# Weight low halves wholly on VectorE for every batch of a decoder layer, with the emission order that follows

## The chip, the cores and the metric

The kernel runs on one NeuronCore of a Trainium2 chip. The metric is the device time of one execution in microseconds; the kernel before has 2865.8 us as the median of three runs (2864.34 to 2872.69). The engines are named as the profile names them: PE is TensorE (its weight loads stand apart as PEld), DVE is VectorE, ACT is ScalarE, POOL is GpSimd, and SP issues all the DMAs.

## The reference, cut to what matters

One decoder layer on 2048 prompt tokens and 8 x 4 sample tokens, in float32. A modulated RMSNorm feeds one input projection; its columns go to three token mixers (SSD, RWKV-7, S5); their outputs are joined and projected, added to the residual, and a second modulated norm feeds a squared-ReLU MLP of width 4096.

```
h    = rmsnorm(x) * (1 + sc1) + sh1
proj = h @ w_in
y    = concat(ssd(proj), rwkv(proj), s5(proj))
x    = x + g1 * (y @ w_out)
h2   = rmsnorm(x) * (1 + sc2) + sh2
x    = x + g2 * (relu(h2 @ w1)**2 @ w2)
```

## The kernel before

Tokens go in four batches b = 0..3 of 512; batch 2 carries the 32 sample tokens too, so its matrix products go in two pieces of 272 columns where the others go in one of 512. Features lie on the partitions. Each large product is made in float32 precision from rounded operands: a weight `w` and an activation `x` are each split into a rounded high half and a low half (`lo = w - hi`), and three matmuls are summed, hi by hi, hi by lo and lo by hi. These are the "GEMM" matmuls of this text; in the rows they read `bk<-arena_r` (`arena_r` is the rounded part of SBUF, `arena` the rest, `bk` a PSUM bank). There are 11,344 such matmuls in the program (64 of them belong to S5) and 2,812 others, mostly float32 and small, which belong to the mixers, the norms and the modulation; "small matmuls" here.

A weight tile of 128 x 1024 comes by one DMA and is used as two halves of 128 x 512. `wprep` has ACT write the high half, `wlow` (line 716) makes the low half. `WS.POOL` says how many of its 512 columns POOL subtracts; the rest is DVE's. It is 288 during all four input projections and for batches 0 and 1 of the second part, and 0 for batches 2 and 3 (line 2538). So 462 halves are split between the two engines: 176 of the input projections and 286 of batches 0 and 1 after them.

The program first does the input projections of the four batches (`in_proj`), and then for each batch the output projection and the MLP (`out_proj0` or `out_proj`, `mlp`). The mixers run as generators beside all of this. The output projection of a batch needs the mixers' output of that batch: it is stored to DRAM tiles named `sph` and read back by `y_gen`, which splits it in two halves for the GEMM.

Nothing reorders the instructions on the chip: each engine runs its list as written. The order is set while the program is written, by `Plan`, which keeps a rough clock for each engine and books a cost for each instruction (in `Eng`). For DVE and POOL it books, for n columns:

```
cost = 72 + 1.04 * n + (30 if ps else 0)                       # DVE
cost = 60 + (2.4 if op == "tensor_tensor" else 0.9) * n        # POOL
```

`pump` (line 314) lets the generators write their next instructions, and passes one over while a booked clock is too far ahead:

```
if max(clk["DVE"], clk["ACT"]) > clk["PE"] + lag or clk["POOL"] > clk["PE"] + 2 * lag:
    continue
```

`gemm` (line 779) calls `wprep` and `wlow` one or two halves ahead of use and calls `pump` after every four matmuls; `wait_for` and `until` pump until a flag is there.

Of the kernel before, what the change touches and what calls it, by code (L numbers as in the profile page):

```python
# [110 lines left out]


class Plan:
    """Rough clocks of the engines while the program is written; they only decide the order in which it is written."""

    LAT = {"PE": 197.0, "DVE": 128.0, "ACT": 143.0, "POOL": 85.0, "SP": 0.0}
    U = 32
# [27 lines left out]

    IDS = {"PE": 1, "DVE": 2, "ACT": 3, "POOL": 4, "SP": 5}

# [41 lines left out]
class Eng:  # L189
# [3 lines left out]
    def __getattr__(self, op):  # L193
# [3 lines left out]
        def call(*a, **k):  # L197
# [34 lines left out]
            elif name == "ACT":  # L232
                cost = 95 + 0.833 * n
            elif name == "POOL":
                cost = 60 + (2.4 if op == "tensor_tensor" else 0.9) * n
# [12 lines left out]
def layer_kernel(ctx: ExitStack, tc: tile.TileContext, d, o, dbg=None):  # L248
    nc = tc.nc
    plan = Plan()  # L250
    V, S, P, T, Q = (Eng(plan, *x) for x in (("DVE", nc.vector), ("ACT", nc.scalar), ("POOL", nc.gpsimd), ("PE", nc.tensor), ("SP", nc.sync)))

# [30 lines left out]

    ctx.enter_context(tc.manual_schedule())

    # ------------------------------------------------------------ plumbing
    gens = []
    done = set()

# [5 lines left out]
    def spawn(g, rank=5, ready=0.0):  # L295
        x = Gen(g, rank)
        x.ready = ready
        gens.append(x)
        gens.sort(key=lambda q: q.rank)
        return x  # L300
# [13 lines left out]
    def pump(budget=1500, idle=False):  # L314
# [3 lines left out]
        while go and clk["PE"] < limit:  # L318
            go = False
            for x in list(gens):  # L320
                if x.ready > clk["PE"] + (60 if idle or x.rank < MRANK else -tune[0]):
                    continue
                lag = LAG1 if x.rank < 0.5 else LAG3 if crit[0] else tune[1]
                if max(clk["DVE"], clk["ACT"]) > clk["PE"] + lag or clk["POOL"] > clk["PE"] + 2 * lag:
                    continue
# [122 lines left out]
    def bc(ap, k, n):  # L448
        return ap.unsqueeze(k).to_broadcast([*ap.shape[:k], n, *ap.shape[k:]])

    # ------------------------------------------------------------ constants
    cst = M.get(C_N)
    vec = M.get(V_N)
    cin = M1.get(72)
# [52 lines left out]
    s5dec = M.get(512)  # L507
    V.memset(s5h.f, 0.0)

    # ------------------------------------------------------------ small helpers  # L510
    def rsqrt(v, n, p=128):
        t_, y_, h_ = (grab(n, AM) for _ in range(3))
        t, y, h = t_.f[0:p], y_.f[0:p], h_.f[0:p]
        ts(t.bitcast(I32), v.bitcast(I32), 1, None, ALU.logical_shift_right)
        ts(h, v, -27.0 / 1024, None, ALU.mult)
        ts(y.bitcast(I32), t.bitcast(I32), -1.0, float(0x5F3759DF), ALU.mult, ALU.add)
        tt(t, y, y, ALU.mult)
        tt(t, t, v, ALU.mult)
        stt(t, t, -10.0 / 3, t, ALU.add, ALU.mult)
        yield 0  # L520
        stt(y, t, 5.0, y, ALU.add, ALU.mult)
        tt(t, y, y, ALU.mult)
        tt(t, t, h, ALU.mult)
        stt(y, t, 0.5625, y, ALU.add, ALU.mult)
        yield 0
        free(t_, h_)
        return y_
# [77 lines left out]
        ts(dv(D_A, 8), dv(D_A, 8), -1.0, None, ALU.mult)  # L605
        done.add("A")

    # ------------------------------------------------------------ adaLN
    mod = M.get(48 * 9)
    modv = mod.v("p (m s) -> p m s", m=48)  # L610
    G1 = M.get(72)
# [68 lines left out]
            yield  # L680
            yield from finish()

    # ------------------------------------------------------------ weights
    NWH = 4
    wring = [(MR.get(512), MR.get(512)) for _ in range(NWH)]
    wbuf = M.get(1024 * NRB)
# [3 lines left out]
    class WS:  # L690
# [1 line left out]
        ready = 0  # L692
        low = 0
        pos = 0
        POOL = 288

    def wload(upto):
        while WS.loaded < min(upto, len(wseq)):
# [5 lines left out]
    def whalves(i):  # L704
        hi, lo = wring[i % NWH]
        return hi, lo, wraw[i // 2 % NRB][:, 512 * (i % 2):512 * (i % 2) + 512]
# [9 lines left out]
    def wlow(upto):  # L716
        while WS.low < min(upto, WS.ready):
            i = WS.low
            hi, lo, raw = whalves(i)
            c = 512 - WS.POOL  # L720
            tt(lo.r[:, 0:c], raw[:, 0:c], hi.f[:, 0:c], ALU.subtract)
# [137 lines left out]
                fn(bk, BT - c0, c1 - c0, BT, True)  # L859
            gput(bk)  # L860

    # ------------------------------------------------------------ token mixers, first stage
    def store(dst, src):
        Q.dma_start(dst, src)

# [307 lines left out]
        ub.free()  # L1173
        done.add(("u", b, i))

    # ------------------------------------------------------------ S5
    LWS = -0.30326532985631671

    def s5_setup():
# [369 lines left out]
        yf.free()  # L1549
        done.add(("s5", b))  # L1550

    # ------------------------------------------------------------ SSD
    def ssd_chunk(b, c):
        smp = c == 4
        n = 32 if smp else 128
# [159 lines left out]
        for c in cs:  # L1715
            yield from admit(ssd_chunk(b, c), C_SSD, R_SSD(b))

    # ------------------------------------------------------------ RWKV, second stage
    def rw_pre(b):
        hasS = b == SB  # L1720
        nch = 9 if hasS else 8
# [370 lines left out]
        if b == SB:  # L2092
            spawn(ssd_gen(b, [4]), R_SMP)

    # ------------------------------------------------------------ main line
    def mix_flags(b):
        fl = [("s5", b)]
        for c in range(5 if b == SB else 4):
            fl += [("ssd", b, c), ("rw", b, c)]
        return fl  # L2100
# [242 lines left out]
    def out_proj0(acts):  # L2343
        xs = []
        for k in range(2):
            load_x(0, k, xs)
        for c in range(4):
            until(("ssd", 0, c))
        wait_for(lambda: len(acts) >= 4, "acts")
        for m in range(8):  # L2350
            if m < 6:
                load_x(0, m + 2, xs)
            resid(xs[m], gemm([(h.r, l.r) for h, l in acts[0:4]], False, acts[0:4] if m == 7 else ()), modv[:, GA1 + m], False)
            pump()
        acc = [mal(W), 0]
        wait_for(lambda: len(acts) == 8, "acts")
        for m in range(8):
            resid(xs[m], gemm([(h.r, l.r) for h, l in acts[4:8]], False, acts[4:8] if m == 7 else ()), modv[:, GA1 + m], False)
            square(xs[m], acc, BT)
            pump()  # L2360
        new = []
        spawn(norm2_gen(xs, acc, False, new), 0)
        return xs, new

    def out_proj(b, acts):
        hasS = b == SB
        n = W if hasS else BT
        xs = []
        for k in range(2):
            load_x(b, k, xs)  # L2370
        for fl in mix_flags(b):
            until(fl)
        acc = [mal(W), 0]
        pair = gemm2(acts, hasS)
        for m in range(8):
            if m < 6:
                load_x(b, m + 2, xs)
            got = next(pair) if m < 2 else gemm([(h.r, l.r) for h, l in acts], hasS, acts if m == 7 else ())
            resid(xs[m], got, modv[:, GA1 + m], hasS)
            square(xs[m], acc, n)  # L2380
            crit[0] = m == 7
            pump()
        new = []
        spawn(norm2_gen(xs, acc, hasS, new), 0)
        return xs, new
# [44 lines left out]
    def w2_chunk(b, xs, hid, ms=range(8), acc=None):  # L2430
        hasS = b == SB
        n = W if hasS else BT
        while tails:
            x = tails.pop(0)
            if x in gens:
                for _ in x.g:
                    pass
                gens.remove(x)
        until(("ada", 23))
        hid = [hid[j] for j in range(4)]  # L2440
        hp = [(h.r, l.r) for h, l in hid]
        for m in ms:
            got = gemm(hp, hasS)
            resid(xs[m], got, modv[:, GA2 + m], hasS)
            if acc is not None:
                square(xs[m], acc, n)
            pump()
        if m == 7:
            for h, l in hid:
                free(h, l)  # L2450
# [31 lines left out]
    def final_gen(b, xs, acc):  # L2482
        hasS = b == SB
        out = []
        while acc[1] < 8:
            yield
        yield
        yield from stats_end(acc[0::2], 1.0 / 1024, 1e-6, hasS, out)
        yield
        yield from bcast_gen(out, hasS)  # L2490
        yield
        bk, b2 = out
        n = W if hasS else BT
        for k in range(8):
            stt(xs[k].f[:, 0:BT], xs[k].f[:, 0:BT], vv(V_GF + k), bk, ALU.mult, ALU.mult)
            if hasS:
                stt(xs[k].f[:, BT:W], xs[k].f[:, BT:W], vv(V_GF + k), b2[:, 0:32], ALU.mult, ALU.mult)
            Q.dma_start(o["y"][k, :, boff[b]:boff[b] + n], xs[k].f[:, 0:n])
            if k % 2:
                yield 0  # L2500
        MB.put(bk)
        if b2 is not None:
            MB.put(b2)
        free(*xs)
        done.add(("final", b))

    # ------------------------------------------------------------ run
    first4 = [4, 0, 5, 1, 6, 2, 7, 3]
    nxt = [[]]
    ys = []  # L2510
# [24 lines left out]
    until(("ada", 11))  # L2535
    last = None
    for b in range(NB):
        WS.POOL = 0 if b > 1 else 288
        tune[:] = MARGIN2, LAG4
        xs, acts = out_proj(b, ys) if b else out_proj0(ys)  # L2540
        for _ in rest:
            pass
        if last is not None:
            w2_chunk(*last[0:3], range(HOLD, 8), last[3])
            spawn(final_gen(last[0], last[1], last[3]), 0.4)
        ys = []
        hid, acc = mlp(b, xs, acts, ys)
        last = (b, xs, hid, acc)
# [11 lines left out]
        dbg(nc, locals())  # L2560


# [1 line left out]
def _consts():  # L2564
    c = np.zeros((128, C_N), np.float32)
    i = np.arange(128)
# [161 lines left out]
```

## Time and profile before

| | |
|---|---|
| median of three runs | 2865.8 us (2864.34 to 2872.69) |
| profiled execution, span from first to last instruction | 2863.7 us |
| PE busy | 2739.5 us, 96% |
| DVE busy | 1967.3 us, 69% |
| ACT busy | 1142.5 us, 40% |
| POOL busy | 653.5 us, 23% |

The profile gives no time beside the span; the median of the runs lies 2.1 us above it. By the time of the first load of `w_out` (`in_w_out`, 785.81 us on SP's queue) the output projection of batch 0 is about to start; POOL has nothing more to do after about 1,950 us. A row of the timeline has a start, a duration, an engine, an operation and its shapes; instructions of one kind that follow each other are merged (x2).

### The profile page before, as it was taken

The numbers are of one execution on the slowest core, as the hardware profiler recorded it, in microseconds if no ns is written. First come the engines' busy times: TensorE is split into PE (matmuls) and PEld (weight loads), VectorE is DVE, ScalarE is ACT, GpSimd is POOL, SyncE is SP. The second block draws the span as 40 slices with busy tenths as digits, with TensorE's granted clock in tenths as the row PEclk, the third lists the DMA queues.
The fourth block names the chain that finished last, engine by engine and source line by source line (L and its number), as shares of the span: only waits on it lengthen the run. The fifth ranks groups of instructions, "written<-read, shape, count | busy, mean of one in ns | idle before, by whom it ended". The sixth has DMA issues, their size and how long they took to land.

```text
span 2863.7 us, 45369 instructions
## 1 busy us (share of the span) xinstructions
PE 2739.5 (96%) x16651; PEld 2265.7 (79%) x16651; DVE 1967.3 (69%) x4567; ACT 1142.5 (40%) x2153; POOL 653.5 (23%) x829
## 2 busy tenths in 40 slices
PE   7999889999999999999999999999999999999997
PEld 4677778877777777777777777778899999888886
DVE  6988996887997877666676778676653535643434
ACT  4354443454335432233443432334534344433342
POOL 1234432233442233322323343321000000000000
PEclk9999999999999999999999999999999999999999
DMA  8467656446553444433434364334222223232222
GB/s 284 155 213 252 201 163 198 164 155 215 170 191 115 144 125 155 146 115 97 159 129 135 118 188 142 120 118 151 96 89 89 89 89 133 82 126 96 99 93 74
DMA packets 302667, 406.26 MB, mean 142 GB/s; under 512 B 85604, under 2 KB 197348, under 8 KB 302444
## 3 DMA queue, kind: packets, MB, share of 16 engines
q1 hardware_dynamic: 302444, 403.36, 42.8%
q8 instruction: 131, 2.15, 0.3%
q14 instruction: 92, 0.75, 0.1%
HBM read 329.67 MB, written 73.62 MB: 141 GB/s over the span
## 4 chain that ended last, share of the span: by engine, by line
PE 62%; DVE 9%; issue 2%; ACT 1%; DMA 1%; POOL 0%; SPq 0%; DVEq 0%; POOLq 0%; ACTq 0%
PE bk L198 62%; DVE arena L198 7%; DVE arena_r L198 2%; ACT arena L198 1%; ACT arena_r L198 1%; DMA arena<-sph 0%; DMA arena<-spk 0%; POOL arena L198 0%; DMA arena<-in_w_out 0%; POOL arena_r L198 0%; DMA arena<-spl 0%; SPq L198 0%; DVEq L198 0%; DVEq L2724 0%; POOLq L198 0%
## 5 line engine op out<-in xcount | busy, mean ns | idle before, releaser
L198 PE MATMUL bk<-arena_r 128*128 128x512 f32 (+1 forms) x11344 | 2284.7, 358 | 61.7 <-DVE arena_r L198 41.5
L198 PEld LDWEIGHTS bk<-arena_r 128*128 128x128 f32 x11344 | 1843.9, 190 | 397.9 <-DVE arena_r L198 65.4
L198 DVE TENSOR_TENSOR arena_r<-arena,arena_r 128x224 fp32r<-128x224 f32 (+2 forms) x981 | 577.7, 610 | 416.9 <-ACT arena_r L198 410.6
L198 ACT ACTIVATE arena_r<-arena 128x512 fp32r<-128x512 f32 (+1 forms) x976 | 581.5, 627 | 468.4 <-PE bk L198 394.3
L198 POOL TENSOR_TENSOR arena_r<-arena,arena_r 128x288 fp32r<-128x288 f32 (+1 forms) x530 | 510.7, 976 | 1055.2 <-ACT arena_r L198 933.2
L198 ACT ACTIVATE arena<-bk 128x512 f32<-128x512 f32 (+8 forms) x619 | 271.9, 459 | 1008.5 <-PE bk L198 798.3
L198 PE MATMUL bk<-arena 128*128 128x128 f32 (+14 forms) x5139 | 540.3, 290 | 50.9 <-DVE arena L198 37.5
L198 PEld LDWEIGHTS bk<-arena 128*128 128x128 f32 (+6 forms) x5139 | 429.7, 152 | 179.7 <-issue 71.2
L198 DVE TENSOR_TENSOR arena<-arena 128x512 f32<-128x512 f32 (+16 forms) x1286 | 515.2, 411 | 51.1 <-ACT arena L198 16.6
L198 DVE SCALAR_TENSOR_TENSOR arena<-bk,arena 128x512 f32<-128x512 f32 (+1 forms) x368 | 235.4, 644 | 269.7 <-PE bk L198 264.0
L198 ACT ACTIVATE arena<-arena 128x512 f32<-128x512 f32 (+4 forms) x445 | 290.1, 664 | 208.1 <-DVE arena L198 189.7
L198 DVE SCALAR_TENSOR_TENSOR arena<-arena 128x512 f32<-128x512 f32 (+9 forms) x605 | 252.2, 430 | 26.6 <-ACT arena L198 6.7
L198 DVE TENSOR_TENSOR arena<-bk,arena 128x512 f32<-128x512 f32 (+4 forms) x277 | 101.2, 381 | 37.0 <-PE bk L198 31.4
L198 POOL TENSOR_TENSOR arena<-arena 128x512 f32<-128x512 f32 (+1 forms) x56 | 73.6, 1320 | 193.5 <-DVE arena L198 100.2
L198 DVE TENSOR_TENSOR arena<-arena,bk 128x512 f32<-128x512 f32 (+2 forms) x163 | 100.4, 627 | 15.3 <-PE bk L198 12.6
L198 DVE SCALAR_TENSOR_TENSOR arena<-arena,bk 64x64 f32<-64x64 f32 (+3 forms) x278 | 91.4, 355 | 27.4 <-PE bk L198 24.1
L198 DVE TENSOR_SCALAR arena<-arena 128x4 f32<-128x4 f32 (+14 forms) x359 | 95.8, 289 | 13.6 <-ACT arena L198 7.8
L198 POOL COPY arena<-arena 128x3 f32<-128x3 f32 (+6 forms) x222 | 70.0, 327 | 47.3 <-ACT arena L198 29.9
L198 ACT ACTIVATE arena<-bk,arena 128x512 f32<-128x512 f32 (+4 forms) x112 | 57.0, 535 | 17.8 <-PE bk L198 16.6
L198 DVE COPY arena<-bk 64x256 f32<-64x256 f32 (+5 forms) x85 | 43.6, 513 | 4.1 <-PE bk L198 2.6
L198 DVE TENSOR_TENSOR_SCAN arena<-arena 128x256 f32<-128x256 f32 (+2 forms) x40 | 36.1, 902 | 1.3
L198 DVE TENSOR_REDUCE arena<-arena 128x4 f32<-128x256 f32 (+1 forms) x34 | 14.0, 412 | 6.7 <-ACT arena L198 6.4
(14 smaller groups left out, 46.3 us busy)
## 6 DMA issues: line engine op xcount, KB each, us to landing
arena<-in_w SPq DMA_DIRECT2D x256, 512.0 KB
arena<-in_w_in SPq DMA_DIRECT2D x88, 512.0 KB
arena<-in_ada_w SPq DMA_DIRECT2D x24, 1024.0 KB
arena<-in_x SPq DMA_DIRECT2D x64, 256.0 KB
arena<-spk SPq DMA_DIRECT2D x32, 512.0 KB
arena<-in_w_out SPq DMA_DIRECT2D x32, 512.0 KB
spk<-arena SPq DMA_DIRECT2D x40, 256.0 KB
spl<-arena SPq DMA_DIRECT2D x33, 256.0 KB
```

What stands on the lines that cost most here:

```text
L198: r = fn(*a, **k)
```

## The change

`WS.POOL` is 0 from the start and the line that set it for each batch is gone, so `c` in `wlow` is 512, DVE makes every low half in one instruction, and POOL makes none. The other lines of the diff take comments out.

```diff
@@ class WS
         ready = 0
         low = 0
         pos = 0
-        POOL = 288
+        POOL = 0
@@ the loop over the batches, second part
     for b in range(NB):
-        WS.POOL = 0 if b > 1 else 288
         tune[:] = MARGIN2, LAG4
         xs, acts = out_proj(b, ys) if b else out_proj0(ys)
```

`wlow`, which reads it, is not edited:

```
c = 512 - WS.POOL
tt(lo.r[:, 0:c], raw[:, 0:c], hi.f[:, 0:c], ALU.subtract)
if c < 512:
    P.tensor_tensor(lo.r[:, c:], raw[:, c:], hi.f[:, c:], ALU.subtract)
```

The bookings of `Plan` change with it: for each of the 462 halves, DVE is booked 1.04 x 288 = 300 ns more and POOL 60 + 2.4 x 288 = 751 ns less. So `pump` decides otherwise from the first projection on, and the order of all engines' lists changes.

DVE's list near its start, where the first five low halves stand (the rows around them belong to the modulation); the difference, with - for before:

```order
 L198 SCALAR_TENSOR_TENSOR arena<-arena 128x18
 L198 TENSOR_TENSOR arena<-bk_71,arena 128x18
-L198 TENSOR_TENSOR arena_r<-arena,arena_r 128x512
-L198 TENSOR_TENSOR arena_r<-arena,arena_r 128x224 x4
+L198 TENSOR_TENSOR arena_r<-arena,arena_r 128x512 x5
 L198 TENSOR_TENSOR arena<-bk_72,arena 128x18
```

The 224-column pieces have become 512-column ones (the first 512 of before is an activation's low half); in POOL's list the 288-column instructions are gone.

PE's list where the output projection of batch 0 starts, before (rows of x24 are tiles of the input projection, rows of x12 the first half of output tiles):

```order
L198 MATMUL bk_66<-arena_r 128x512 x24
L198 MATMUL bk_67<-arena_r 128x512 x24
L198 MATMUL bk_65<-arena_r 128x512 x24
L198 MATMUL bk_66<-arena_r 128x512 x24
L198 MATMUL bk_67<-arena_r 128x512 x12
L198 MATMUL bk_65<-arena_r 128x512 x12
```

and in the changed kernel, from the end of the last tile of the input projection (its last 12 matmuls), of the stretch that follows the first rows alone:

```order
L198 MATMUL bk_65<-arena_r 128x512 x12
L198 MATMUL bk_69<-arena 32x2x64 x8
L198 MATMUL bk_68<-arena 128x8
L198 MATMUL bk_72<-arena 64x128 x8
L198 MATMUL bk_70<-arena 32x2x64 x8
L198 MATMUL bk_71<-arena 64x128 x8
L198 MATMUL bk_68<-arena 128x128 x4
L198 MATMUL bk_69<-arena 32x2x64 x8
L198 MATMUL bk_72<-arena 128x256 x2
L198 MATMUL bk_68<-arena 64x128 x8
```

The stretch goes on to 93 small matmuls and four more from `arena_r` of the mixers before the first output tile follows (`bk_66<-arena_r 128x512 x8`); before, output tiles followed projection tiles with nothing in between. In DVE's list 104 instructions stand in that stretch.

SP's list where the mixers' output of batch 0 (`sph_109`) is read back, before:

```order
L198 DMA sph_109<-arena 128x4x128
L198 DMA arena<-in_w_in 128x1024
L198 DMA spk_82<-arena 128x8x64
L198 DMA spg_86<-arena 128x512
L198 DMA arena<-spf_98 128x512 x2
L198 DMA spf_100<-arena 128x512
L198 DMA arena<-in_w_in 128x1024
L198 DMA arena<-sph_109 128x512 x4
L198 DMA arena<-spg_85 128x4x128
L198 DMA arena<-spx_74 128x8x128
L198 DMA arena<-in_w_in 128x1024
```

and in the changed kernel:

```order
L198 DMA sph_109<-arena 128x2x128
L198 DMA spk_82<-arena 128x8x64
L198 DMA spg_86<-arena 128x512
L198 DMA arena<-spf_98 128x512 x2
L198 DMA sph_109<-arena 128x4x128
L198 DMA arena<-spg_85 128x4x128
L198 DMA arena<-sph_109 128x512 x4
L198 DMA arena<-spx_74 128x8x128
L198 DMA arena<-sph_109 128x512 x2
L198 DMA sph_109<-arena 128x2x128
L198 DMA spk_82<-arena 128x8x64
L198 DMA arena<-sph_109 128x512 x2
```

Before, the loads stand among loads of `in_w_in`, in the middle of the last input projection; now they stand after three loads of `in_w_out`, when no load of `in_w_in` is left.

Counted over PE's list, the small matmuls stand like this (of 2,812 in both):

| part of the program, by GEMM matmuls passed | before | changed |
|---|---|---|
| input projections of batches 0, 1, 2 | 254 + 178 + 367 = 799 | 139 + 179 + 153 = 471 |
| input projection of batch 3 | 280 | 418 |
| output projection of batch 0 | 85 | 194 |
| MLP of batch 0 | 904 | 734 |
| batch 1, second part | 670 | 597 |
| batch 2, output projection and MLP | 8 + 27 = 35 | 160 + 199 = 359 |
| batch 3 and the end | 39 | 39 |

## Rows read from the trace of the kernel before

**Rows 1.** The page: busy time and share of each engine.
```profile
PE 2739.5 (96%) x16651; PEld 2265.7 (79%) x16651; DVE 1967.3 (69%) x4567; ACT 1142.5 (40%) x2153; POOL 653.5 (23%) x829
```
**Rows 2.** Stretches: bounds, length, busy us of PE, PEld, DVE, ACT, POOL, granted clock, DMA.
```profile
0.00:200.00 200.00, 173.63 (x1011) 126.57 (x1012) 161.13 (x452) 101.24 (x181) 55.56 (x86) 0.97 0.63 213
200.00:360.00 160.00, 146.63 (x789) 112.47 (x788) 142.55 (x346) 68.75 (x124) 65.81 (x90) 0.97 0.71 228
360.00:600.00 240.00, 224.14 (x1796) 197.86 (x1796) 200.53 (x503) 107.56 (x255) 82.30 (x132) 0.97 0.53 172
600.00:800.00 200.00, 190.69 (x1140) 146.98 (x1139) 168.35 (x383) 81.88 (x160) 69.77 (x97) 0.99 0.60 192
800.00:2110.00 1310.00, 1272.30 (x7584) 1027.73 (x7583) 939.83 (x2184) 497.06 (x920) 380.04 (x424) 0.99 0.41 134
2110.00:2780.00 670.00, 663.71 (x4041) 598.82 (x4041) 315.75 (x635) 261.76 (x479) 0.00 (x0) 0.99 0.29 99
```
**Rows 3.** Waits of PE, 0 to 800 us: us in total, times, longest.
```profile
PE bk L198 <- DVE arena L198: 29.4, 10, 13.8
PE bk L198 <- DVE arena_r L198: 23.3, 22, 3.2
```
**Rows 4.** Waits of PE, 800 to 2,110 us.
```profile
PE bk L198 <- DVE arena_r L198: 16.8, 21, 3.9
PE bk L198 <- ACT arena_r L198: 9.5, 4, 3.6
PE bk L198 <- DVE arena L198: 4.9, 7, 1.6
```
**Rows 5.** Groups by form, whole span: count, busy us, mean ns, idle before.
```profile
L198 POOL TENSOR_TENSOR arena_r<-arena,arena_r 128x288 fp32r<-128x288 f32 x462 | 436.3, 952 | 1037.0 <-ACT arena_r L198 933.2 <-PE bk L198 56.6 <-DMA arena<-in_x 17.4
L198 DVE TENSOR_TENSOR arena_r<-arena,arena_r 128x512 fp32r<-128x512 f32 x458 | 320.3, 720 | 264.3 <-ACT arena_r L198 263.4 <-issue 0.2
L198 DVE TENSOR_TENSOR arena_r<-arena,arena_r 128x224 fp32r<-128x224 f32 x462 | 224.2, 489 | 120.8 <-ACT arena_r L198 116.0 <-DMA arena<-spg 3.1
L198 DVE SCALAR_TENSOR_TENSOR arena<-arena 128x512 f32<-128x512 f32 x176 | 146.6, 840 | 9.0 <-ACT arena L198 4.5 <-PE bk L198 0.9 <-POOL arena L198 0.8
L198 DVE TENSOR_TENSOR arena<-arena 128x512 f32<-128x512 f32 x155 | 118.6, 767 | 3.1 <-ACT arena L198 0.7
L198 DVE TENSOR_TENSOR arena<-arena 128x4 f32<-128x4 f32 x260 | 66.4, 262 | 9.6
```
**Rows 6.** Groups by form on DVE, 2,100 to 2,400 us.
```profile
L198 DVE TENSOR_TENSOR arena_r<-arena,arena_r 128x512 fp32r<-128x512 f32 x99 | 65.8, 686 | 97.9 <-ACT arena_r L198 97.9
```
**Rows 7.** Groups by form on DVE, 2,450 to 2,800 us.
```profile
L198 DVE SCALAR_TENSOR_TENSOR arena<-bk,arena 128x512 f32<-128x512 f32 x57 | 42.7, 750 | 72.4 <-PE bk L198 72.4
...
L198 DVE TENSOR_TENSOR arena<-arena 128x512 f32<-128x512 f32 x2 | 1.4, 692 | 0.2
...
L198 DVE TENSOR_TENSOR arena<-arena 128x4 f32<-128x4 f32 x4 | 0.6, 162 | 0.1
```
**Rows 8.** Timeline, 302 to 326 us, DVE and POOL: start, duration, what.
```profile
322.07 0.39 DVE L198 TENSOR_TENSOR arena_r<-arena,arena_r 128x224 fp32r<-128x224 f32 x1
...
325.30 1.01 POOL L198 TENSOR_TENSOR arena_r<-arena,arena_r 128x288 fp32r<-128x288 f32 x1 [6.70 <-ACT arena_r L198]
325.57 1.30 DVE L198 TENSOR_TENSOR arena<-arena 128x512 f32<-128x512 f32 x1
```
**Rows 9.** The page: the group of small matmuls from `arena`.
```profile
L198 PE MATMUL bk<-arena 128*128 128x128 f32 (+14 forms) x5139 | 540.3, 290 | 50.9 <-DVE arena L198 37.5
```
**Rows 10.** Timeline of SP's queue around the loads of `sph`.
```profile
652.49 0.36 SPq L198 DMA_DIRECT2D sph<-arena  x1
...
657.81 2.46 SPq L198 DMA_DIRECT2D arena<-sph  x4
...
697.59 0.98 SPq L198 DMA_DIRECT2D arena<-sph  x2
```
**Rows 11.** Timeline of SP's queue, the first load of `w_out`.
```profile
785.81 0.38 SPq L198 DMA_DIRECT2D arena<-in_w_out  x1
```
**Rows 12.** Stretches, columns as in rows 2.
```profile
815.00:850.00 35.00, 31.06 (x134) 25.10 (x134) 30.80 (x74) 9.76 (x16) 13.31 (x16) 0.90 0.40 122
930.00:1360.00 430.00, 424.56 (x2634) 332.27 (x2630) 306.10 (x733) 153.07 (x295) 133.88 (x141) 1.00 0.41 130
1900.00:2110.00 210.00, 202.57 (x1402) 185.25 (x1401) 131.74 (x328) 85.77 (x160) 16.00 (x18) 0.98 0.35 121
2110.00:2440.00 330.00, 328.06 (x2534) 323.29 (x2534) 158.77 (x360) 127.27 (x253) 0.00 (x0) 1.00 0.29 100
```

## Prediction

> **What bounds the kernel now.** I read the page's busy times first [rows 1]: PE is busy 2739.5 of 2863.7 us, so 124 us are all that any change off PE can give back, and the change takes no work from PE. Then the stretches [rows 2]: PE is not equally full. In the first 800 us, which are the four input projections, it is busy 173.63 + 146.63 + 224.14 + 190.69 = 735.1 us, so 65 us are idle there; from 800 to 2,110 us 38 are, and from 2,110 to 2,780 only 6. DVE lies the other way: 89% busy from 200 to 360 us, 84% from 600 to 800, and 47% from 2,110 to 2,780. The waits say the same [rows 3, 4]: before 800 us PE waits 29.4 + 23.3 = 52.7 us for DVE, of which 13.8 are one wait (I take it to be the first norm, at the start); after that 16.8 + 4.9 = 21.7 us. So the reader is to see a kernel bound by PE, whose losses come where DVE is dense and PE waits for a result at the end of DVE's list.
>
> **What the change takes away and adds on DVE and POOL.** POOL loses 462 instructions of 952 ns, 436.3 us of its 653.5 [rows 1, 5]. DVE loses 462 of 489 ns, 224.2 us, and gets 462 of 512 columns. Their price: the same form takes 686 ns from 2,100 to 2,400 us [rows 6], where POOL does nothing, and 720 ns over the whole span. I take 686, because most of POOL's work is gone: 462 x 0.686 = 316.9 us, so DVE gains 92.7 us.
>
> Something comes back, for DVE's instructions are longer beside POOL's. A 224-column low half takes 0.39 us when alone [rows 8] and 489 ns in the mean [rows 5]; in one place a 512-column instruction that starts 0.27 us after POOL's takes 1.30 us and ends 0.56 us after POOL's end [rows 8], where the like takes 692 ns without POOL [rows 7]. By form, mean against the mean without POOL [rows 5 to 7]: 260 x (262 - 162) = 26 us, 458 x (720 - 686) = 16, 155 x (767 - 692) = 12, and 176 x (840 - 750) = 16, the last against the nearest row, one with a PSUM input. That is 70 us, of which I give the low halves POOL's share, 436.3/653.5 = 0.67: 47 us. So DVE's busy time would rise by 93 - 47 = 46 us; forms that I did not price give back more, so I expect 2,000 us of busy time, between 1,930 (they give back twice as much) and 2,060 (nothing comes back). A low half is ready sooner: one instruction of 0.69 us in place of the later end of 0.49 and 0.95 us.
>
> The Trainium skill bears on this: "SBUF — State Buffer", § Who interferes with whom, states that a VectorE instruction with two SBUF inputs and a GpSimd instruction that reads SBUF cannot run at once, and that the second waits for the first to end. The trace agrees (1.30 us against 0.69) [rows 7, 8]. Taken to its end the rule makes of the removed instructions a gain on every DVE chain, which is the first rival.
>
> **What moves.** The planner books 300 ns more on DVE for each half, in all 462 x 0.3 = 138 us, and knows nothing of the 47 us or more that come back, so `pump` sees DVE as too far ahead more often and holds the mixers. Counted in the lists, 799 - 471 = 328 small matmuls leave the first three projections; 138 of these go to the fourth, 109 to the output projection of batch 0, and with the 243 that leave the MLP of batch 0 and batch 1, 324 go to batch 2, where DVE is half idle. PE's work stays the same: 5,139 records for small matmuls take 540.3 us [rows 9], or about 0.19 us for each of the program's 2,812.
>
> 1. *First three projections.* 41% of the small matmuls leave, and their DVE work with them. PE's waits for DVE there, without the first one, are 52.7 - 13.8 = 38.9 us [rows 3]. I take 41% of these: -16 us. Bounds: 0 (the low halves now fill DVE instead) and -35 (nearly all go).
>
> 2. *Start of the output projection of batch 0.* This is the new wait. Before, the mixers' output of batch 0 is read back at 657.81 to 697.59 us [rows 10], and `w_out`'s first load is issued at 785.81 us [rows 11]: some 90 us of margin. Now PE's list holds 93 small matmuls with no GEMM among them before the first output tile, and DVE's list 104 instructions beside them, so the projection waits for the mixers' ends. Behind PE's wait stand all the GEMMs. DVE's part: 104 x 0.262 us (the small form, rows 5) = 27 us to 104 x 168.35/383 = 104 x 0.44 us (the mean of 600 to 800 us, rows 2) = 46 us. PE's own work in it is 93 x 0.19 = 18 us, which it has anyway. So 9 to 28 us are idle; I take 18. The store to `sph` is issued at 652.49 and the loads that need it 5.3 us later [rows 10]; in the new place these 5.3 us lie partly under DVE's other work and I add nothing, but keep 5 as an upper end. Then the clock: in the one comparable stretch, where PE waits for a norm, it was granted 0.90 of the full 2.4 GHz over 35 us [rows 12], 3.5 us. In all +21 us, between +8 and +37.
>
> 3. *Fourth projection.* From 600 to 800 us PE is idle 9.3 us with DVE at 84% [rows 2]. With half as many small matmuls again, DVE fills up further. I add two thirds of that idle time, +6 us, between 0 and +15.
>
> 4. *800 to 2,110 us.* Fewer small matmuls, quicker DVE instructions. Of the 21.7 us of waits for DVE [rows 4] I take a fifth off: -4 us, between -12 and 0.
>
> 5. *Batch 2.* 359 small matmuls where 35 were. From 930 to 1,360 us, equally dense with mixers, PE is idle 1.3% of the time; from 1,900 to 2,110 us 3.5%, and in the pure GEMMs of 2,110 to 2,440 us 0.6% [rows 12]. The 324 more are 62 us of PE's work, in some 250 us of the program: 1.3% of that is +3 us, between 0 and 8.
>
> Sum: -16 + 21 + 6 - 4 + 3 = +10 us on the profiled span of 2863.7, so 2874 us; the median of the runs lies 2.1 us above that span, so 2876 us. ACT's work and the DMAs stay the same in number; the DMA engines are busy 29% to 71% of the time [rows 2 and 12], so the later loads cost nothing by themselves. POOL's remaining work (scans and decay products of the mixers) no longer queues behind low halves; it stood on PE's waits nowhere in rows 3 and 4, and I count it at nothing.
>
> **Rivals.**
>
> *A: the freed port wins.* POOL's instructions stood in DVE's way all through the dense stretches; without them the small DVE steps of a chain fall from 262 to 162 ns [rows 5, 7]. For it speaks that 52.7 + 21.7 = 74 of PE's 124 idle us are waits for DVE [rows 3, 4]. Against it, that DVE has 93 us more of its own, and that the new wait in term 2 stands in the lists whatever the port does. If the waits of rows 3 fall by three quarters (-29), those of rows 4 by half (-11), and the new wait has its low end (+8), the time is 2863.7 - 32 + 2 = 2834 us; with half of the first two it is 2863.7 - 12 + 2 = 2854 us. I take 2844.
>
> *B: DVE becomes the engine that decides.* The mechanism is one: the fourth projection and the start of the output projection of batch 0 hold 418 + 194 small matmuls in place of 280 + 85, and DVE, at 84% there already, cannot carry their work beside two low halves in each tile. It decides from the point where DVE's busy share passes some 95%. Then terms 2 and 3 have their upper ends, 37 + 15, and the first three projections gain nothing: 2863.7 + 52 - 4 + 3 + 2 = 2917 us. For it: PE already loses time there, and each stall costs clock too [rows 12]. Against it: the first three projections are thinner in any case, and DVE's other instructions there get shorter. The Trainium skill, "Perfetto Trace Analysis", § Optimizing Scalar/DVE Operations, says that work may be moved to GpSimd when DVE is saturated, and that this may not help because of the shared read port. By its first half the change is wrong where DVE is at 89% and right at 47%; by its second it is neutral. The 46 us worked out above lie in between.
>
> *C: nothing decides.* PE's work is the same to the instruction and its idle time moves from one place to another: -16 against +21 cancel within their bounds, 2866 us.
>
> **How the numbers follow.** My forecast (the new wait outweighs the thinner projections by a little) has 0.45, and by itself 2862 to 2892 us; A 0.27, B 0.18, C 0.10. The prediction is the forecast's 2876 us. The range reaches up to B's upper part and down to A's middle: 2846 to 2912 us leaves out about 2 in 10. What a measurement of this kernel can tell from no change is about 0.3%, here 2857.2 to 2874.4 us. Slower: 0.27 of the forecast's 0.45, B's 0.18 and 0.02 of C, 0.47. Faster: 0.24 of A, 0.01 of the forecast, 0.01 of C, 0.26. The same: what is left, 0.27.
>
> **What would show it.** DVE's low halves read 128x512 with about 920 in place of 458, at about 0.69 us; the 288-column form is gone and POOL is busy about 217 us; DVE about 2,000. Term 1: PE's waits for DVE in the first three projections fall to some 23 us beside the first one. Term 2: right after the last load of `in_w_in`, a stretch of 27 to 46 us in which PE runs small matmuls alone and is idle 9 to 28 us, then a clock below 1. Term 5: small matmuls among the 272-column GEMMs, PE still above 98%. The prediction is wrong if the wait in term 2 is short because DVE had been ahead, or if PE's idle time before it falls by more than 21 us.

## The result, and the profile after

The changed kernel takes 2838.61 us in the median of 4 runs (2836.94 to 2842.76), the kernel before 2867.43 us (2864.34 to 2872.69). The ratio is 0.9896, with a 95% interval from 0.9878 to 0.9914: 1.0% faster, where 2876 us had been forecast. The time lies just below the predicted range, on the side of rival A, the freed port. The profiled execution of the changed kernel has a span of 2837.7 us.

The page's busy line after, beside [rows 1]:

```profile
PE 2730.4 (96%) x16651; PEld 2274.3 (80%) x16651; DVE 1923.9 (68%) x4567; ACT 1144.1 (40%) x2153; POOL 223.1 (8%) x367
```

DVE does more work than before, in the same number of instructions, and is busy 43.4 us *less* (1967.3 before). POOL falls by 430.4 us, as its 436.3 us of low halves go. PE falls by 9.1 us with the same instructions.

The stretches after, with the columns of [rows 2] (bounds, length, busy us of PE, PEld, DVE, ACT, POOL, granted clock, DMA); the last two rows are the two new waits that are spoken of below:

```profile
0.00:200.00 200.00, 178.53 (x1012) 133.99 (x1013) 152.62 (x444) 102.43 (x183) 12.80 (x43) 0.95 0.61 208
200.00:360.00 160.00, 154.43 (x811) 122.76 (x810) 119.82 (x315) 80.84 (x154) 14.73 (x43) 0.99 0.63 202
360.00:600.00 240.00, 234.45 (x1812) 206.40 (x1811) 194.34 (x496) 106.09 (x245) 48.42 (x101) 1.00 0.64 206
600.00:800.00 200.00, 186.10 (x1161) 140.29 (x1160) 168.87 (x402) 79.39 (x152) 24.90 (x37) 0.91 0.59 184
800.00:2110.00 1310.00, 1270.47 (x7730) 1042.51 (x7729) 946.30 (x2240) 500.18 (x927) 122.25 (x145) 0.98 0.42 134
2110.00:2780.00 670.00, 664.04 (x3948) 594.19 (x3948) 316.07 (x627) 259.35 (x470) 0.00 (x0) 0.99 0.31 99
718.00:756.00 38.00, 27.75 (x125) 18.52 (x125) 33.87 (x93) 13.72 (x27) 6.00 (x6) 0.59 0.51 147
1955.00:1980.00 25.00, 11.07 (x53) 9.42 (x52) 20.69 (x55) 15.33 (x25) 0.61 (x1) 0.66 0.08 27
```

The stretches are equal in time and not in work: the third projection ends at 616 us before and at 504 us now, with fewer small matmuls done. Up to 600 us PE was idle 26.4 + 13.4 + 15.9 = 55.7 us before [rows 2] and is idle 21.5 + 5.6 + 5.6 = 32.7 us now, and the clock is 0.99 and 1.00 where it was 0.97 from 200 to 600 us (before that 0.95 against 0.97). DVE from 200 to 360 us is at 75% instead of 89%. From 600 to 800 us the new wait shows: PE idles 13.9 us instead of 9.3, and the clock falls to 0.91. After that little changes.

The waits of PE after, 0 to 800 us (us in total, times, longest), beside [rows 3]:

```profile
PE bk L198 <- DVE arena L198: 24.3, 6, 13.9
PE bk L198 <- ACT arena_r L198: 7.8, 4, 2.7
PE bk L198 <- DVE arena_r L198: 4.6, 6, 1.4
```

And from 800 to 2,110 us, beside [rows 4]:

```profile
PE bk L198 <- ACT arena_r L198: 19.3, 3, 13.9
PE bk L198 <- DVE arena_r L198: 8.7, 9, 2.4
PE bk L198 <- DVE arena L198: 6.5, 6, 2.4
```

PE's waits for low halves (`arena_r` of DVE) fall from 23.3 to 4.6 us in the first stretch and from 16.8 to 8.7 in the second. One wait for ACT of 13.9 us is new.

The groups by form after, beside [rows 5] (count, busy us, mean ns of one, idle before):

```profile
L198 DVE TENSOR_TENSOR arena_r<-arena,arena_r 128x512 fp32r<-128x512 f32 x920 | 623.7, 696 | 396.0 <-ACT arena_r L198 385.7 <-DMA out_s_ssd<-arena 4.7 <-DMA arena<-in_w_out 1.6
L198 DVE SCALAR_TENSOR_TENSOR arena<-arena 128x512 f32<-128x512 f32 x176 | 131.8, 759 | 15.2 <-ACT arena L198 11.2 <-PE bk L198 1.4 <-POOL arena L198 0.3
L198 DVE TENSOR_TENSOR arena<-arena 128x512 f32<-128x512 f32 x155 | 111.1, 721 | 3.5 <-ACT arena L198 1.3
L198 DVE TENSOR_TENSOR arena<-arena 128x4 f32<-128x4 f32 x260 | 48.1, 191 | 11.3 <-POOL arena L198 1.8
```

Each of these four forms, which DVE had before too, is shorter in the mean: 720 to 696 ns, 840 to 759, 767 to 721, 262 to 191. All four read two operands from SBUF. A form that reads one of its two tensors from a PSUM bank did not change at all, first before, then after:

```profile
L198 DVE SCALAR_TENSOR_TENSOR arena<-bk,arena 128x512 f32<-128x512 f32 x224 | 167.3, 747 | 200.0 <-PE bk L198 199.1
L198 DVE SCALAR_TENSOR_TENSOR arena<-bk,arena 128x512 f32<-128x512 f32 x224 | 167.3, 747 | 188.8 <-PE bk L198 188.3
```

### The profile page after: what moved, and what is told of

Read it like the earlier page. It is cut to its first block, busy times and chain, and to the rows that moved or that the text cites. A ratio compares the mean times of both kernels' runs of the same rounds, so it can differ in the third digit from the quotient of the medians.

```text
span 2837.7 us, 44420 instructions
## 1 busy us (share of the span) xinstructions
PE 2730.4 (96%) x16651; PEld 2274.3 (80%) x16651; DVE 1923.9 (68%) x4567; ACT 1144.1 (40%) x2153; POOL 223.1 (8%) x367
## 5 line engine op out<-in xcount | busy, mean ns | idle before, releaser
L198 DVE TENSOR_TENSOR arena_r<-arena,arena_r 128x512 fp32r<-128x512 f32 (+2 forms) x981 | 661.7, 695 | 424.2 <-ACT arena_r L198 413.4
L198 DVE TENSOR_TENSOR arena<-arena 128x4 f32<-128x4 f32 (+20 forms) x1286 | 442.5, 354 | 44.1 <-ACT arena L198 9.1
L198 ACT ACTIVATE arena<-arena 128x512 f32<-128x512 f32 (+6 forms) x445 | 289.7, 664 | 146.4 <-DVE arena L198 130.0
L198 DVE SCALAR_TENSOR_TENSOR arena<-arena 128x512 f32<-128x512 f32 (+10 forms) x605 | 225.4, 386 | 33.0 <-ACT arena L198 16.9
L198 DVE TENSOR_TENSOR arena<-bk,arena 128x512 f32<-128x512 f32 (+5 forms) x277 | 101.7, 381 | 52.8 <-PE bk L198 41.7
L198 DVE TENSOR_TENSOR arena<-arena,bk 128x512 f32<-128x512 f32 (+4 forms) x163 | 100.6, 628 | 21.7 <-PE bk L198 13.2
L198 POOL COPY arena<-arena 128x8 f32<-128x8 f32 (+5 forms) x222 | 63.2, 311 | 655.9 <-ACT arena L198 546.5
L198 POOL TENSOR_TENSOR arena_r<-arena,arena_r 128x512 fp32r<-128x512 f32 (+1 forms) x68 | 76.5, 1145 | 458.9 <-PE bk L198 458.8
L198 DVE TENSOR_SCALAR arena<-arena 128x4 f32<-128x4 f32 (+15 forms) x359 | 76.1, 235 | 14.2 <-ACT arena L198 8.5
L198 ACT ACTIVATE arena<-bk,arena 128x512 f32<-128x512 f32 (+4 forms) x112 | 57.1, 535 | 24.0 <-PE bk L198 15.9
```

The source lines that it names most:

```text
L198: r = fn(*a, **k)
```

## The experiments

The change has two parts that the diff does not show apart: which engine does the 288 columns, and which durations the planner books, from which the lists' order follows. The theory (P) was that the POOL instructions that are gone had lengthened DVE's, and that this alone makes the kernel faster; the rival (O), that the new lists do. The edits below are cut to the lines that matter; from e6 on the bookings are left out, except where they are the edit.

### The instructions and the lists apart (e1, e2, e3)

**e1_old_order_dve**: all low halves on DVE, booked as before, so that each engine's list stays as it was, apart from POOL's.

```
-        tt(lo.r[:, 0:c], raw[:, 0:c], hi.f[:, 0:c], ALU.subtract)
-        if c < 512:
-            P.tensor_tensor(lo.r[:, c:], raw[:, c:], hi.f[:, c:], ALU.subtract)
+        nc.vector.tensor_tensor(lo.r, raw, hi.f, ALU.subtract)
+        plan.run("DVE", 72 + 1.04 * c, [lo.r[:, 0:c]], [raw[:, 0:c], hi.f[:, 0:c]])
+        if c < 512:
+            plan.run("POOL", 60 + 2.4 * (512 - c), [lo.r[:, c:]], [raw[:, c:], hi.f[:, c:]])
```

> All low halves on VectorE as in the changed kernel, but the planner is booked the old costs (224 columns on VectorE, 288 on GpSimd), so every engine's list stands as before. Theory P (the freed port): the gain comes with the instructions, whatever the order: ratio to the kernel before about 0.990, 2838 us, PE's idle time before 800 us down from 65 to about 40 us. Rival O (the order): the list of before keeps its time, ratio 0.997 to 1.003; the gain needs the mixers moved out of the first projections.

Measured: 2830.18 us, ratio 0.9866 [0.9844, 0.9888]. The instructions alone bring all of the gain. Its page's busy line:

```profile
PE 2729.9 (97%) x16651; PEld 2262.7 (80%) x16651; DVE 1937.4 (69%) x4567; ACT 1141.5 (40%) x2153; POOL 226.9 (8%) x367
```

Its stretch up to the first load of `w_out`, then the same stretch of the kernel before:

```profile
0.00:754.00 754.00, 710.53 (x4678) 566.12 (x4679) 628.15 (x1648) 351.62 (x704) 107.29 (x227) 0.99 0.63 205
```

```profile
0.00:786.00 786.00, 722.16 (x4676) 573.95 (x4677) 659.08 (x1651) 352.35 (x703) 268.87 (x401) 0.97 0.60 197
```

The same PE work takes 32 us less, of the 36.1 us by which the whole span is shorter: PE's idle time falls from 63.8 to 43.5 us, its busy time from 722.2 to 710.5 at a clock of 0.99 instead of 0.97, and DVE's busy time by 30.9 us although it does more.

**e2_new_order_split**: the split as before, with the whole 512 columns booked on DVE, so that the lists are those of the changed kernel.

```
+        nc.vector.tensor_tensor(lo.r[:, 0:c], raw[:, 0:c], hi.f[:, 0:c], ALU.subtract)
+        if c < 512:
+            nc.gpsimd.tensor_tensor(lo.r[:, c:], raw[:, c:], hi.f[:, c:], ALU.subtract)
+        plan.run("DVE", 72 + 1.04 * 512, [lo.r], [raw, hi.f])
```

> The low halves split over both engines as before, but the planner is booked 512 columns on VectorE, so every engine's list stands as in the changed kernel. Theory P: the stall at the first output projection is there and nothing is given back: slower than before, ratio 1.000 to 1.010. Rival O: the order alone brings the gain: ratio about 0.990 (0.987 to 0.994).

Measured: 2869.99 us, ratio 1.000 [0.999, 1.001]. The new lists bring nothing by themselves; O falls.

**e3_dummy_pool**: the changed kernel, in which POOL besides does a useless subtraction of 288 columns at each of the 462 halves. It reads what it used to read and writes to a tile that nobody reads.

```
+        if WS.POOL:
+            nc.gpsimd.tensor_tensor(junk[:, :], raw[:, 224:], hi.f[:, 224:], ALU.subtract)
```

> The changed kernel's lists to the row on PE, VectorE, ScalarE and SP, and beside each of the 462 low halves GpSimd computes 288 columns that nobody reads, from the same operands. VectorE's work is that of the changed kernel; only the interference is back. Theory P: VectorE's busy time rises from 1924 us by some 150 us or more and the time goes to 1.000 or above. Rival O: under 0.3% more than the changed kernel, ratio 0.990 to 0.993.

Measured: 2943.74 us, ratio 1.0261 [1.0244, 1.0279], 3.7% above the changed kernel. The page's busy line:

```profile
PE 2769.5 (94%) x16651; PEld 2291.9 (78%) x16651; DVE 2097.1 (71%) x4567; ACT 1144.7 (39%) x2153; POOL 700.4 (24%) x829
```

Its groups by form (line 721 issues the 462 low halves and the 290 that were whole before, line 724 the useless work):

```profile
L721 DVE TENSOR_TENSOR arena_r<-arena,arena_r 128x512 fp32r<-128x512 f32 x752 | 553.0, 743 | 294.3 <-ACT arena_r L198 285.4 <-DMA out_s_ssd<-arena 4.7 <-DMA arena<-in_w_out 1.6
L724 POOL TENSOR_TENSOR junk<-arena,arena_r 128x288 f32<-128x288 f32 x462 | 466.3, 1009 | 989.4 <-issue 641.7 <-ACT arena_r L198 323.5 <-ACT arena L198 6.2
```

Nobody reads its result, but it holds the halves and weights that it reads a little longer: SP's queue waits 20.9 us for it in the whole span, and ACT 19.7 us:

```profile
ACT arena_r L198 <- POOL junk L724: 19.7, 10, 4.7
```

Such a wait lies before an instruction and not within it. DVE's busy time rises by 173.2 us over the changed kernel's, or 0.37 us for each of the 462. The 3.7% of time may hold a part of those waits besides. PE's waits for low halves in the whole span, then those for all of DVE's `arena_r` in the changed kernel:

```profile
PE bk L198 <- DVE arena_r L721: 56.1, 46, 4.5
```

```profile
PE bk L198 <- DVE arena_r L198: 14.4, 18, 2.4
```

### Reading or writing (e11)

**e11_pool_memset**: as e3, but POOL only writes.

```
+        if WS.POOL:
+            for _ in range(3):
+                nc.gpsimd.memset(junk[:, :], 0.0)
```

> The changed kernel's lists, and beside each of the 462 low halves GpSimd writes zeros to 288 columns that nobody reads, three times, without reading anything. If GpSimd's reads are what blocks VectorE: VectorE's 128x512 low halves stay at 0.69 to 0.71 us, VectorE's busy time within 20 us of 1924, ratio 0.989 to 0.992. If any GpSimd instruction interferes: VectorE's busy time up by 100 us or more, ratio over 1.00.

Measured: 2843.77 us, ratio 0.991 [0.9887, 0.9932], which can't be told from the changed kernel. Groups by form:

```profile
L721 DVE TENSOR_TENSOR arena_r<-arena,arena_r 128x512 fp32r<-128x512 f32 x752 | 516.2, 694 | 316.3 <-ACT arena_r L198 313.0 <-DMA arena<-in_w_out 1.6
L725 POOL MEMSET junk<- 128x288 f32 x1386 | 472.1, 341 | 72.4 <-POOLq L2723 0.3
```

POOL is busy as long as in e3 (472.1 us against 466.3), and DVE's instruction keeps its 694 ns against 743 there. The memsets also run in the same stretches: 160 us of them before 600 us against 152 us of e3's work, and 279 from 800 to 2,110 us against 285. What costs DVE is that POOL reads. The Trainium skill, "SBUF — State Buffer", § Who interferes with whom, says just this: a VectorE instruction with two SBUF inputs contends with a GpSimd instruction that reads SBUF, and not with one that only writes it. The trace agrees in both halves. That sentence does not cover all that was seen: TENSOR_SCALAR, which has one tensor input, takes 95.8 us before, 76.1 in the changed kernel and 80.6 beside the memsets; those 4.5 us are most of the 6.8 by which DVE is busier here (1930.7 us against 1923.9).

### Where it pays (e6, e7, e4, e8, e9)

**e6_old_order_proj** and **e7_old_order_second**: e1 for one part of the halves alone, under the old lists. e6 takes the 178 halves that are made before the output projection of batch 0 begins (176 of the four projections, and 2 for `w_out` that are made ahead), e7 the other 284.

```
+        k = 512 if WS.PROJ else c         # e7: if not WS.PROJ
+        nc.vector.tensor_tensor(lo.r[:, 0:k], raw[:, 0:k], hi.f[:, 0:k], ALU.subtract)
+        if k < 512:
+            nc.gpsimd.tensor_tensor(lo.r[:, k:], raw[:, k:], hi.f[:, k:], ALU.subtract)
```

> Lists as before on every engine; the 176 halves of the input projections are VectorE's alone, the 286 of batches 0 and 1 after them stay split. Theory P1 (the interference costs where VectorE is dense): nearly the whole gain of the run with all 462 halves on VectorE and the old lists (ratio 0.9866): 0.987 to 0.990. Rival P2 (every removed GpSimd instruction gives the same, 38 us over 462): 176/462 of it, ratio 0.994 to 0.996.

> The reverse: lists as before, the halves of the input projections split, those of batches 0 and 1 after them VectorE's alone. P1: ratio 0.997 to 1.000. P2: 286/462 of the gain, 0.991 to 0.993.

Measured: e6 2841.62 us, 0.9898 [0.9878, 0.9919]; e7 2860.48 us, 0.9967 [0.9953, 0.998]. The two add up to e1: -1.02 - 0.33 = -1.35% against -1.34%. Per half, the projections' are worth 1.02/178 = 0.0057% and the others 0.33/284 = 0.0012%. e7 lies at the edge of what was expected of it (0.997 to 1.000). It pays most in the projections, where DVE is dense [rows 2]; what else differs between the two parts was not separated. The first load of `w_out`, which stands at the same place of SP's list in all of these, says where (785.81 us before [rows 11]; here e6, then e7):

```profile
750.27 0.50 SPq L198 DMA_DIRECT2D arena<-in_w_out  x1
```

```profile
787.31 0.38 SPq L198 DMA_DIRECT2D arena<-in_w_out  x1
```

**e4_proj_only**: the same part as e6, but booked as it is done, which gives the projections the changed kernel's new lists.

```
-        POOL = 288
+        POOL = 0                  # the last line stays: WS.POOL = 0 if b > 1 else 288
```

> GpSimd gets no low halves in the input projections and its 288 columns again for batches 0 and 1 after them. Theory P: the projections hold 176 of 462 halves and 65 of 103 idle us of PE, so half to three quarters of the gain: ratio 0.992 to 0.996. Rival O: about the same by its order; it expects the later two thirds of the halves to matter nothing: ratio 0.989 to 0.991.

Measured: 2868.51 us, 0.9996 [0.9985, 1.0008]. This missed what was expected: e6's 1.0% is lost when the lists move too.

**e8_old_then_new** and **e9_new_then_old**: all halves on DVE, and one part alone of the lists new: e8 from the output projection of batch 0 on, e9 in the projections.

```
         nc.vector.tensor_tensor(lo.r, raw, hi.f, ALU.subtract)    # booked as in e1
+        POOL = 0                  # e9: class WS
+        WS.POOL = 0               # e8: at the first use in the loop over batches
```

> All low halves on VectorE; the planner is booked the old costs during the input projections, the new ones after them. If the 8 us that the new lists lose against the old ones (0.9896 against 0.9866) come from the thin projections and the wait at the first output projection, this runs as the old lists do: ratio 0.985 to 0.987, 2822 to 2830 us. If they come from the lists after the projections (the wait of 13.9 us at the MLP of batch 2), ratio 0.988 to 0.990.

> All low halves on VectorE; the planner is booked the new costs during the input projections and the old ones after them, the reverse of the run that kept the old lists through the projections (0.9872). If the lists of the projections carry the 8 us that the changed kernel lies behind the old lists: ratio 0.989 to 0.991. If the later lists do: 0.986 to 0.988.

Measured: e8 2833.47 us, 0.9872 [0.9846, 0.9898]; e9 2845.41 us, 0.9917 [0.9893, 0.9941]. So the new lists of the projections, with the wait behind them, cost 0.9917/0.9872, or 0.45% (13 us, with an uncertainty of 0.34%), and the later ones nothing that can be seen. That is a net: up to the end of the third projection PE idles 39.4 us in e8 and 30.1 in e9, and behind it 63.1 and 82.8. e4 and e9 have the same lists on PE, ACT and SP and differ in the 284 later halves alone: these are worth 0.8% there, against the 0.33% of e7 (the difference has an uncertainty of about 0.3%). A gain measured under one order is not the gain under another.

### Further on the same way (e12, e13)

**e12_decay_dve**: e1, and 68 decay products of the mixers (64 of them 128x512) moved from POOL to DVE too, booked as before. If DVE's sum decides (theory D), this costs; if each reading POOL instruction that goes is a gain (G), it is faster still.

```
-            P.tensor_tensor(Rv[k], ...)
+            nc.vector.tensor_tensor(Rv[k], ...)
+            plan.run("POOL", 60 + 2.4 * 4 * n, ...)
```

> The old lists and all low halves on VectorE (ratio 0.9866), and 68 more of GpSimd's instructions, the products of 128x512 for the decay matrices of SSD (1.19 us each), go to VectorE at the place where GpSimd had them. Price by the low halves: a GpSimd instruction of 0.95 us cost VectorE 123/462 = 0.27 us, so these cost it 0.33 us each, 23 us, and at 0.69 us each they add 47. Theory D (VectorE's busy time decides, and only what gives back more than it adds pays): VectorE +24 us, ratio 0.990 to 0.997. Rival G (every read that GpSimd no longer makes is a gain): ratio 0.982 to 0.986.

Measured: 2820.24 us, 0.9828 [0.9804, 0.9853]. The page's busy line:

```profile
PE 2717.5 (97%) x16651; PEld 2256.8 (80%) x16651; DVE 1946.0 (69%) x4635; ACT 1141.6 (41%) x2153; POOL 144.0 (5%) x299
```

The moved products, by form:

```profile
L1575 DVE TENSOR_TENSOR arena_r<-arena,arena_r 128x512 fp32r<-128x512 f32 x64 | 41.0, 681 | 1.3 <-PE bk L198 1.2
```

The first load of `w_out` on SP's queue:

```profile
745.27 0.41 SPq L198 DMA_DIRECT2D arena<-in_w_out  x1
```

DVE takes 41.0 us of the 64 large products alone and is busy only 8.6 us more than in e1; the kernel is another 0.4% faster (with an uncertainty of 0.3%), although DVE's sum rose. D falls. Whether it is POOL's reads alone was not told apart: the product itself is also ready sooner, in 681 ns where POOL took 1,258 in e1.

**e13_all_dve**: e12, and POOL's last 56 products of two inputs moved to DVE in the same way.

> As the run with the decay products on VectorE (ratio 0.9828, old lists), and the last 56 two-input products of GpSimd (40 of 128x512, 1.23 us, and 16 of 504 strided columns, 1.83 us: S5 and the SSD state) go to VectorE too; GpSimd keeps copies and memsets alone. Theory G (a read that GpSimd no longer makes is a gain, also where VectorE's own sum rises): ratio 0.978 to 0.982. Rival D2 (what VectorE adds, 56 x 0.69 = 39 us, now outweighs what comes back, some 25 us): ratio 0.983 to 0.990.

Measured: 2820.21 us, 0.9824 [0.9807, 0.984], the same as e12. The page's busy line:

```profile
PE 2731.0 (97%) x16651; PEld 2265.0 (80%) x16651; DVE 1954.9 (69%) x4691; ACT 1142.5 (41%) x2153; POOL 73.6 (3%) x243
```

Whether these last products still bring anything was not settled. e12 and e13 are 1.7% faster than the kernel before and 0.7% faster than the changed one.

## Why the prediction was wrong, step by step

**The step that failed is "What the change takes away and adds on DVE and POOL".** It held what DVE gets back to 47 us and some 13 more for forms without a price (2,013 to 2,000 us), and the sum of times has no term for it beside a part of term 4. What DVE gains was right: 462 x 0.696 - 224.2 = 97.3 us, forecast 92.7. As DVE's sum fell by 43.4 us, 97.3 + 43.4 = 141 us came back (131 of them with the lists of before, e1), and DVE's 1923.9 us lie below the lower end of 1930. The four forms that were priced behaved as priced: 18.3 + 11 + 7.5 + 14.8 = 52 us of change [rows 5]. The other 89 us are in forms that were not priced, some forty of them, of which 128x256 with two SBUF inputs gave most (75.9 to 65.5 us). The prediction priced single forms, where the page groups all forms of an operation. The page's groups before:

```profile
L198 DVE TENSOR_TENSOR arena<-arena 128x512 f32<-128x512 f32 (+16 forms) x1286 | 515.2, 411 | 51.1 <-ACT arena L198 16.6
L198 DVE SCALAR_TENSOR_TENSOR arena<-arena 128x512 f32<-128x512 f32 (+9 forms) x605 | 252.2, 430 | 26.6 <-ACT arena L198 6.7
L198 DVE TENSOR_SCALAR arena<-arena 128x4 f32<-128x4 f32 (+14 forms) x359 | 95.8, 289 | 13.6 <-ACT arena L198 7.8
```

and after:

```profile
L198 DVE TENSOR_TENSOR arena<-arena 128x4 f32<-128x4 f32 (+20 forms) x1286 | 442.5, 354 | 44.1 <-ACT arena L198 9.1
L198 DVE SCALAR_TENSOR_TENSOR arena<-arena 128x512 f32<-128x512 f32 (+10 forms) x605 | 225.4, 386 | 33.0 <-ACT arena L198 16.9
L198 DVE TENSOR_SCALAR arena<-arena 128x4 f32<-128x4 f32 (+15 forms) x359 | 76.1, 235 | 14.2 <-ACT arena L198 8.5
```

These three alone fall by 72.7 + 26.8 + 19.7 = 119 us, of which 41 are in priced forms. Taking 0.67 of the difference, as POOL's share, did little harm: it gave 47 us for the priced forms, and 52 came. The price in time is e1's: 1.34%, some 38 us, with the lists untouched.

**Term 1 (first three projections, -16 us)** was right in its size and in its cause, and only one of two gains there. The third projection ends with the last of its 1,056 matmuls of 272 columns. PE up to there, before, in e2 (new lists, split halves), in e1 (old lists, whole halves) and in the changed kernel (columns as in rows 2):

```profile
0.00:616.00 616.00, 560.40 (x3725) 450.69 (x3726) 516.62 (x1325) 284.37 (x573) 205.32 (x310) 0.97 0.62 203
```

```profile
0.00:522.00 522.00, 483.00 (x3041) 397.05 (x3041) 409.50 (x1051) 256.21 (x511) 187.76 (x291) 0.96 0.60 199
```

```profile
0.00:589.00 589.00, 548.95 (x3727) 442.65 (x3728) 490.79 (x1323) 283.64 (x573) 79.23 (x176) 0.99 0.64 210
```

```profile
0.00:504.00 504.00, 475.44 (x3039) 392.94 (x3040) 388.55 (x1052) 255.80 (x511) 58.80 (x157) 0.98 0.63 207
```

PE's idle time is 55.6 us before and 39.0 in e2: the mixers' leaving alone brings 16.6 us. It is 40.1 us in e1: the instructions alone bring about as much, and for them the sum had no term. Both together bring it to 28.6 us. These 27 us are more than the 21 that the prediction had named as a sign of its being wrong. On top of the waits came 11.6 us of PE's busy time in e1 up to the first load of `w_out`, at the higher clock, which no term held.

**Term 2 (the new wait at the output projection of batch 0, +21 us)** is there. PE's timeline after (start, duration, what, and in brackets the idle time before it):

```profile
721.53 11.51 PE L198 MATMUL bk<-arena 128*128 128x256 f32 x64
734.87 4.79 PE L198 MATMUL bk<-arena 128*128 128x128 f32 x16 [1.83 <-DVE arena L198]
744.43 0.66 PE L198 MATMUL bk<-arena 128*128 128x128 f32 x2 [4.78 <-DVE arena L198]
747.05 1.87 PE L198 MATMUL bk<-arena 128*128 128x2 f32 x8 [1.96 <-ACT arena L198]
748.78 1.20 PE L198 MATMUL bk<-arena_r 128*128 128x512 f32 x2
```

From 718 to 756 us PE is idle 10.3 us (9 to 28 forecast) with DVE at 89%, and the granted clock is 0.59 of 2.4 GHz in the mean, so most of the stretch passes at the lower level of 1.2. At the upper one the 27.75 us that PE is busy there would be up to 11 us shorter (27.75 x 0.41, an estimate). The forecast had 18 us of idle time and 3.5 for the clock, so its 21 us are near the mark by two errors that cancel. The loads of `sph`, 90 us early before [rows 10], now come last:

```profile
677.26 0.43 SPq L198 DMA_DIRECT2D arena<-in_w_out  x1
...
739.16 1.76 SPq L198 DMA_DIRECT2D arena<-sph  x4
...
752.01 1.02 SPq L198 DMA_DIRECT2D arena<-sph  x2
```

**Term 3 (fourth projection, +6 us)** did not come: beside the wait, PE idles 13.9 - 10.3 = 3.6 us from 600 to 800 us, and 5.6 in the 240 us before.

**Term 4 (-4 us)** was right in its direction, 21.7 - 15.2 = 6.5 us less waiting for DVE. **Term 5 (+3 us)** was too low: where the MLP of batch 2 begins, the second norm now ends late. PE after, and the same place before:

```profile
1974.20 0.82 PE L198 MATMUL bk<-arena_r 128*128 128x272 f32 x2 [13.93 <-ACT arena_r L198]
```

```profile
2037.65 7.61 PE L198 MATMUL bk<-arena_r 128*128 128x272 f32 x35 [3.02 <-ACT arena_r L198]
```

That is 11 us more, at a clock of 0.66, in a place to which the prediction had given 0 to 8. The lists make it: the wait is 13.9 us in e2 too, and 3.0 in e1.

**The sum.** The five terms, read as the price of the new lists, came to +10 us. Measured, the lists cost 0.9896/0.9866, or 0.3% (9 us, with an uncertainty of about as much), with all halves on DVE, and nothing beside POOL's (e2). What was missing is e1's -38 us: with it the sum is 2863.7 + 10 - 38 + 2 = 2838 us. That it comes so near to the 2838.61 measured is in part luck, as the errors of terms 3 and 5 cancel. Of the rivals, A had the mechanism and 2844 us; B's wait exists and does not decide, with DVE at 84% from 600 to 800 us and 89% in the wait, below the 95% that B asked for; C falls.

**What stays open.** How 30 us of DVE become 38 us of time was followed to PE's idle time (-20) and busy time (-12 at the higher clock) before the first load of `w_out`, and not through each chain. That a low half in one piece is ready sooner may have a part in it, which was not measured apart; e3, where it is also done in one piece, is slower than e2 with the same lists (2943.74 us against 2869.99), so it brings no net gain while POOL goes on reading.

## What to carry to other kernels

Work on GpSimd that reads SBUF is paid for by the VectorE instructions beside it that read two operands there, in relation most by the short ones (27% on 128x4, 3 to 10% on 128x512); price it by the sums of all groups of that engine and not by its largest forms, and look at the stretch where that engine is dense. A change that also alters what a planner books is two changes: run each with the other held. Here the instructions were worth 1.3% and the order lost some 0.3% (with an uncertainty as large), so the better of the two took the new instructions and kept the old order.

## What was not expected of the hardware

A GpSimd instruction that reads 288 columns for 0.95 us cost VectorE 131 us / 462 = 0.28 us in the mean (e1: 462 x 0.703 - 224.2 + 29.9 = 131 us), and in e3, beside whole low halves, 0.37 us. Memsets that keep GpSimd busy as long cost VectorE 6.8 us in all and no time that can be told. The Trainium skill, "Perfetto Trace Analysis", § Optimizing Scalar/DVE Operations, holds here in its second half (moving work between these two may not help) and not in its first (that it may make sense when VectorE is saturated): at 89% of VectorE [rows 2] the work was still better taken back.
